# Top-k masks from one pass of signs: a change to the mask chain of a hybrid encoder kernel

## The chip, the cores and the metric

The kernel runs on one core of a Trainium2 chip. The metric is the device time of one execution in microseconds (us). TensorE is PE in the profile, its weight load PEld, VectorE is DVE, ScalarE is ACT, GpSimd is POOL, and SP issues the DMAs.

## The reference

The reference is an encoder trunk of two layers over 1024 tokens of width 1024, f32. Each layer has a token mixer (a gated convolution, six heads of sparse attention chosen by an indexer, six heads of chunked band attention), a cross-attention to 256 memory tokens, and a squared-ReLU MLP, each behind a layer norm. The change touches the choice of keys in the sparse attention:

```python
score = jnp.einsum('bqh,bqhs->bqs', iwb, jax.nn.relu(logits)).astype(jnp.float32)
admissible = key_chunk[None, :] <= q_chunk[:, None]
score = jnp.where(admissible[None], score, -jnp.inf)
_, idx = lax.top_k(score, topk)        # topk = 256 keys per query
...
s = jnp.einsum('bqhd,bqkd->bhqk', qb, k_sel).astype(jnp.float32) * scale
p = jax.nn.softmax(s, axis=-1)
```

Of equal scores, the top-k takes those with the lower index.

## The kernel before

Queries are worked in eight blocks of 128, one query per partition. Block b may see keys 0 to 128(b+1) - 1, so its scores have w = 128(b+1) columns. Blocks 0 and 1 see at most 256 keys and need no choice; blocks 2 to 7 (w = 384 to 1024) do.

The kernel keeps all keys and adds a mask before the softmax: 0 where a key is chosen, 2^100 (`BIG`) where not. `softmax` (L964) works on negated scores, takes the minimum of score plus mask along the way out of PSUM (L977), and applies Exp on ScalarE (L983).

`topk` (L761) makes the masks. It finds each query's threshold bit by bit, 32 rounds. Two groups of blocks are searched side by side: group 0 (blocks 7 and 6) counts on ScalarE, as the sum of Sign(threshold - score) (L789); group 1 (blocks 5 to 2) counts on VectorE (L793). Then the masks are made block by block, the narrowest first: 384, 512, 640, 768, 896 and 1024 columns. For the two blocks of group 0 some instructions ahead (L828 to L843) correct the threshold. Then, for every block:

- `eq` = BIG where the score equals the threshold (L845);
- the scores are overwritten by 1 where they are at or below the threshold, with their count (L848, whose accumulator is read by an instruction of its own);
- `need`, the number of equal scores still to be taken, times BIG (L853);
- `pre`, the running sum of `eq` (L856, a scan);
- `eq` is cleared where the running sum exceeds `need` (L857);
- the mask is written in bf16 over the scores' buffer (L860).

All are VectorE instructions. A block's mask is first read when sparse attention reaches that block, which is behind all 24 units of chunked attention.

Around it, `build` runs two streams side by side: the indexer followed by `topk`, and the projections, the convolution (L940, L943), and then the attention units. The instructions are put in order by the Tile framework's scheduler, by priorities: `topk` is emitted with a priority shifted by 3000 and the indexer by -2000. The order of each engine's queue is fixed when the kernel is compiled. `chunk_prepare` gets a head's queries and keys ready for chunked attention (ScalarE L1012 and L1021, VectorE L1013, GpSimd L1022, two DMAs L1017 and L1018 between halves of partitions, and the bias by a DMA, L1009, negated at L1026), its scores are made by L1054 and leave the two score banks through L977. Buffers in SBUF come from one arena of 52736 columns of 4 bytes, which gives out the place freed longest ago. Weights are loaded ahead by SP, cast on ScalarE (L285) and split on GpSimd (L286). L340 to L342 are the three matmuls of a product in split f32.

Of the kernel before, what the change touches and what calls it, by code (L numbers as in the profile page):

```python
# [15 lines left out]
BF16 = mybir.dt.bfloat16  # L16
I32 = mybir.dt.int32
AF = mybir.ActivationFunctionType
ALU = mybir.AluOpType
# [3 lines left out]
S = 1024  # L23
# [9 lines left out]
TOPK = 256  # L33
# [4 lines left out]
BIG = 2.0**100  # L38
# [272 lines left out]
class Kern:  # L311
# [449 lines left out]
    def topk(self, st):  # L761


        nc, sb = self.nc, self.sb


        groups = GROUPS
        junk, junk_a = sb.alloc(512), sb.alloc(512)
        tmp = [sb.alloc(S) for _ in range(2)]
        junkb = junk.ap.bitcast(BF16)  # L770
        junka = junk_a.ap.bitcast(BF16)
        col = sb.alloc(len(groups) * 32)
        state = []
        for g, blocks in enumerate(groups):

            state.append(
                [col.ap[:, g * 32 + 8 * i : g * 32 + 8 * i + len(blocks)] for i in range(3)]
            )
            nc.gpsimd.memset(state[g][0], 0.0)

        for bit in range(31, -1, -1):
            for g, blocks in enumerate(groups):
                cand, gone, cnt = state[g]
                ci, gi = cand.bitcast(I32), gone.bitcast(I32)
                for j, b in enumerate(blocks):
                    w = (b + 1) * P
                    x, c, n = st["score"][b].ap, cand[:, j : j + 1], cnt[:, j : j + 1]
                    if g == 0:
                        nc.scalar.activation(  # L789
                            junka[:, :w], x, AF.Sign, bias=c, scale=-1.0, accum_out=n  # L790
                        )
                    else:
                        nc.vector.tensor_scalar(  # L793
                            junkb[:, :w], x, c, None, op0=ALU.is_ge, op1=ALU.add, accum_out=n
                        )

                back = -1.0 if bit == 31 else float(1 << bit)
                if g == 0:
                    for j, b in enumerate(blocks):
                        nc.vector.tensor_scalar(  # L800
                            gi[:, j : j + 1], cnt[:, j : j + 1],
                            float((b + 1) * P - 2 * TOPK), back, op0=ALU.is_gt, op1=ALU.mult,
                        )
                else:
                    nc.vector.tensor_scalar(
                        gi, cnt, float(TOPK), back, op0=ALU.is_lt, op1=ALU.mult
                    )

                if bit == 31:
                    nc.vector.tensor_scalar(ci, gi, 1 << 30, None, op0=ALU.bitwise_xor)  # L810
                else:
                    nc.vector.scalar_tensor_tensor(  # L812
                        ci, gi, 1 << (bit - 1) if bit else 0, ci,
                        op0=ALU.bitwise_xor, op1=ALU.bitwise_xor,
                    )
                yield TP * len(blocks) / 4
        for g, blocks in list(enumerate(groups))[::-1]:
            fl, cnt = state[g][0], state[g][2]
            for j, b in list(enumerate(blocks))[::-1]:
                w = (b + 1) * P  # L820
                sc = st["score"][b]
                tcol = fl[:, j : j + 1]
                eq, pre = (x.ap[:, :w] for x in tmp)
                if g == 0:


                    above, more = self.small(1), self.small(1)
                    nc.vector.tensor_scalar(  # L828
                        eq, sc.ap, tcol, None, op0=ALU.is_gt, op1=ALU.add,
                        accum_out=cnt[:, j : j + 1],  # L830
                    )
                    nc.vector.tensor_scalar(
                        eq, eq, -HIGH, HIGH, op0=ALU.mult, op1=ALU.add
                    )
                    nc.vector.tensor_tensor_reduce(
                        pre, sc.ap, eq, 1.0, HIGH, op0=ALU.add, op1=ALU.min,
                        accum_out=above,
                    )
                    nc.vector.tensor_scalar(
                        more.bitcast(I32), cnt[:, j : j + 1], float(TOPK), None,  # L840
                        op0=ALU.is_ge,
                    )
                    nc.vector.copy_predicated(tcol, more.bitcast(I32), above)  # L843

                nc.vector.tensor_scalar(  # L845
                    eq, sc.ap, tcol, BIG, op0=ALU.is_equal, op1=ALU.mult
                )
                nc.vector.tensor_scalar(  # L848
                    sc.ap, sc.ap, tcol, None, op0=ALU.is_le, op1=ALU.add,
                    accum_out=cnt[:, j : j + 1],  # L850
                )
                need = self.small(1)
                nc.vector.tensor_scalar(  # L853
                    need, cnt[:, j : j + 1], float(TOPK - w), BIG, op0=ALU.add, op1=ALU.mult
                )
                nc.vector.tensor_tensor_scan(pre, eq, eq, 0.0, op0=ALU.add, op1=ALU.max)  # L856
                nc.vector.scalar_tensor_tensor(  # L857
                    eq, pre, need, eq, op0=ALU.is_le, op1=ALU.mult
                )
                nc.vector.scalar_tensor_tensor(  # L860
                    sc.mask, sc.ap, BIG, eq, op0=ALU.mult, op1=ALU.subtract
                )
                sb.free(sc.high, self.w.late)
                yield 4.0
        for x in [junk, junk_a, col] + tmp:
            sb.free(x, self.w.late)

    def dsa_proj(self, l, xt, st):
# [1230 lines left out]
```

## Time and profile before

| what | value |
|---|---|
| median of 3 runs | 3052.46 us (3051.95 to 3061.31) |
| the profiled execution | 3054.18 us |
| its span on the core | 3052.4 us |
| mean granted TensorE clock | 0.973 |
| PE busy | 2894.9 us, 95% |
| DVE busy | 2239.0 us, 73% |
| ACT busy | 1527.2 us, 50% |
| POOL busy | 1317.6 us, 43% |

The span is that of the profiled execution, from its first instruction to its last; its own time is 1.8 us longer. Busy shares are means over the whole span. The mask chains run from 267 to 331 us in the first layer and from 1788 to 1858 us in the second.

### The profile page before, as it was taken

What the parts mean: (1) busy time and instruction counts of PE and PEld (TensorE: products, weight loads), DVE (VectorE), ACT (ScalarE), POOL (GpSimd) and SP (SyncE); (2) the same over time, 40 slices, a digit from 0 to 9 for tenths busy, and PEclk for the clock granted to TensorE, in tenths of its full rate; (3) what the DMA queues carried; (4) which work ended last, traced back from release to release, by engine and by line L of the source; (5) the groups of instructions that cost most, each with busy time, mean ns of one, the idle gap of its engine ahead of it and who ended that gap; (6) DMA issues with size and microseconds to landing.
All of it is one profiled execution on the core that took longest, in us unless ns stands there. A gap on an engine that the chain in (4) does not pass through costs nothing. (4 is left out here: it accounts for less than half of the span.)

```text
span 3052.4 us, 43458 instructions
## 1 busy us (share of the span) xinstructions
PE 2894.9 (95%) x14440; PEld 2452.0 (80%) x14440; DVE 2239.0 (73%) x4423; ACT 1527.2 (50%) x3074; POOL 1317.6 (43%) x1260
## 2 busy tenths in 40 slices
PE   8998799999999999999998987999999999999998
PEld 7886688878877788888787866887888777888886
DVE  5899978672478776777858998785725877667787
ACT  5676766513324455544456757665232344554442
POOL 4615566522335553232455154665223355532223
PEclk9999899999999999999999998999999999999999
DMA  3212133331325446755322121323312354466553
GB/s 125 55 43 57 50 102 113 116 114 39 105 101 175 165 154 223 247 186 189 123 71 55 39 65 41 116 93 125 114 52 101 110 174 162 152 249 227 182 180 115
DMA packets 261890, 374.14 MB, mean 123 GB/s; under 512 B 22560, under 2 KB 141344, under 8 KB 261664
## 3 DMA queue, kind: packets, MB, share of 16 engines
q1 hardware_dynamic: 261664, 371.35, 37.0%
q8 instruction: 114, 1.87, 0.2%
q14 instruction: 112, 0.92, 0.1%
HBM read 269.56 MB, written 95.42 MB: 120 GB/s over the span
## 5 line engine op out<-in xcount | busy, mean ns | idle before, releaser
L340 PE MATMUL banks<-sb,sb 128*128 128x512 f32 (+3 forms) x3776 | 1427.2, 379 | 31.8 <-DVE sb L645 11.7
L341 PE MATMUL banks<-sb,sb 128*128 128x512 f32 (+3 forms) x3776 | 1421.4, 377 | 6.0 <-POOL sb L286 5.9
L342 PE MATMUL banks<-sb,sb 128*128 128x512 f32 (+3 forms) x3776 | 1419.5, 377 | 6.5 <-POOL sb L645 6.5
L645 POOL TENSOR_TENSOR sb<-sb,sb 128x512 fp32r<-128x512 f32 (+1 forms) x428 | 588.1, 1386 | 946.1 <-ACT sb L644 834.9
L340 PEld LDWEIGHTS banks<-sb,sb 128*128 128x128 f32 x3776 | 717.0, 190 | 164.0 <-DVE sb L645 14.9
L342 PEld LDWEIGHTS banks<-sb,sb 128*128 128x128 f32 x3776 | 717.1, 190 | 132.0 <-POOL sb L645 7.3
L341 PEld LDWEIGHTS banks<-sb,sb 128*128 128x128 f32 x3776 | 717.6, 190 | 128.7 <-POOL sb L286 7.5
L644 ACT CAST sb<-sb 128x512 fp32r<-128x512 f32 (+1 forms) x788 | 452.5, 605 | 580.1 <-PE banks L341 135.1
L286 POOL TENSOR_TENSOR sb<-sb,sb 128x512 fp32r<-128x512 f32 (+2 forms) x288 | 376.3, 1319 | 512.0 <-ACT sb L285 403.7
L645 DVE TENSOR_TENSOR sb<-sb,sb 128x512 fp32r<-128x512 f32 x360 | 285.8, 821 | 41.6 <-ACT sb L644 41.3
L645 DVE TENSOR_TENSOR sb<-banks,sb 128x384 fp32r<-128x384 f32 (+2 forms) x324 | 187.8, 595 | 80.8 <-ACT sb L644 76.1
L644 ACT CAST sb<-banks 128x384 fp32r<-128x384 f32 (+2 forms) x324 | 160.0, 516 | 172.1 <-PE banks L1521 75.2
L793 DVE TENSOR_SCALAR_CACHE_REDUCE sb<-sb,sb 128x768 bf16<-128x768 f32 (+3 forms) x256 | 207.5, 811 | 4.9 <-POOL sb L749 2.3
L1685 DVE TENSOR_TENSOR sb<-sb,sb 128x512 f32<-128x512 f32 x160 | 158.4, 1025 | 56.9 <-ACT sb L1665 53.9
L1727 DVE TENSOR_TENSOR sb<-banks,sb 128x512 f32<-128x512 f32 x224 | 149.8, 683 | 45.9 <-PE banks L342 40.4
L983 ACT ACTIVATE sb<-sb,sb 128x640 f32<-128x640 f32 (+7 forms) x192 | 141.7, 739 | 77.5 <-DVE sb L977 73.2
L285 ACT CAST sb<-sb 128x512 fp32r<-128x512 f32 (+2 forms) x192 | 112.0, 599 | 125.9 <-PE banks L341 29.2
L994 POOL TENSOR_SCALAR sb<-sb,sb 128x128 f32<-128x128 f32 (+7 forms) x192 | 144.9, 770 | 66.6 <-DVE sb L992 60.6
L789 ACT ACTIVATE sb<-sb,sb 128x1024 bf16<-128x1024 f32 (+1 forms) x128 | 140.3, 1096 | 51.6 <-DVE sb L812 46.8
L1790 DVE TENSOR_TENSOR sb<-sb,sb 128x512 f32<-128x512 f32 x128 | 97.9, 767 | 70.5 <-DMA sb<-w_ff_dram 69.8
L1664 ACT ACTIVATE sb<-sb 128x512 f32<-128x512 f32 x128 | 80.7, 631 | 123.7 <-DVE sb L1727 123.5
L1582 DVE TENSOR_TENSOR sb<-sb,sb 128x512 f32<-128x512 f32 x96 | 91.6, 954 | 50.7 <-DMA h<-sb 30.7
(173 smaller groups left out, 3128.1 us busy)
## 6 DMA issues: line engine op xcount, KB each, us to landing
sb<-h SPq DMA_DIRECT2D x236, 256.0 KB, 3.1
h<-sb SPq DMA_DIRECT2D x224, 256.0 KB, 2.1
sb<-w_ff_dram SPq DMA_DIRECT2D x216, 256.0 KB, 3.1
sb<-w_ff_dram SPq DMA_DIRECT2D x64, 512.0 KB, 4.4
sb<-w_in_dram SPq DMA_DIRECT2D x64, 256.0 KB, 2.8
sb<-w_mkv_dram SPq DMA_DIRECT2D x64, 256.0 KB, 2.7
xs<-sb SPq DMA_DIRECT2D x24, 512.0 KB, 2.6
sb<-xs SPq DMA_DIRECT2D x24, 512.0 KB, 3.8
```

The lines of the kernel that those rows point to most:

```text
L286: k.nc.gpsimd.tensor_tensor(lo, st, hi.bitcast(F32), op=ALU.subtract)
L340: mm(out, lh, rh, start=start, stop=False)
L341: mm(out, lh, rl, start=False, stop=False)
L342: mm(out, ll, rh, start=False, stop=stop)
L644: nc.scalar.copy(hi, src)
L645: eng.tensor_tensor(lo, src, hi.bitcast(F32), op=ALU.subtract)
L789: nc.scalar.activation(junka[:, :w], x, AF.Sign, bias=c, scale=-1.0, accum_out=n)
L793: nc.vector.tensor_scalar(junkb[:, :w], x, c, None, op0=ALU.is_ge, op1=ALU.add, accum_out=n)
L983: nc.scalar.activation(pt.ap, pt.ap, AF.Exp, bias=mn, scale=-1.0, accum_out=sm)
L994: nc.gpsimd.tensor_scalar(pt.ap, pt.ap, rc[:, i : i + 1], 0.0, op0=ALU.mult, op1=ALU.add)
L1685: nc.vector.tensor_tensor(z.ap, x, y, op=ALU.add if spec[1] == "+" else ALU.subtract)
L1727: nc.vector.tensor_tensor(r.ap, ps.ap, part[c, x].ap, op=ALU.add)
```

## The change

The chain from the corrected threshold on is replaced. One pass on ScalarE writes the signs of (threshold - score) in bf16, +1 below the threshold, 0 at it, -1 above, and their sum. VectorE then makes 1 where the sign is 0 (bf16), its running sum, and 4096 times the sign plus the running sum; one comparison of that with `need` writes the mask. `need`, now without BIG, is computed by two one-column instructions from the last running sum and the total of the signs. The scores are no longer overwritten before the mask is. Two buffers of 512 columns, for signs and equalities, are held for as long as `topk` runs, and serve all blocks in turn.

```diff
@@ topk
         tmp = [sb.alloc(S) for _ in range(2)]
+        half = [sb.alloc(512) for _ in range(2)]
...
+                side, same = (x.bitcast(BF16)[:, :w] for x in (half[0].ap, half[1].ap))
+                total, need = self.small(1), self.small(1)
+                nc.scalar.activation(
+                    side, sc.ap, AF.Sign, bias=tcol, scale=-1.0, accum_out=total
+                )
+                nc.vector.tensor_scalar(same, side, 0.0, None, op0=ALU.is_equal)
+                nc.vector.tensor_tensor_scan(pre, same, same, 0.0, op0=ALU.add, op1=ALU.max)
+
                 nc.vector.tensor_scalar(
-                    eq, sc.ap, tcol, BIG, op0=ALU.is_equal, op1=ALU.mult
+                    need, pre[:, w - 1 : w], total, 0.5, op0=ALU.add, op1=ALU.mult
+                )
+                nc.vector.tensor_scalar(need, need, float(TOPK - w // 2), None, op0=ALU.add)
+                nc.vector.scalar_tensor_tensor(
+                    pre, side, 4.0 * S, pre, op0=ALU.mult, op1=ALU.add
                 )
                 nc.vector.tensor_scalar(
-                    sc.ap, sc.ap, tcol, None, op0=ALU.is_le, op1=ALU.add,
-                    accum_out=cnt[:, j : j + 1],
-                )
-                need = self.small(1)
-                nc.vector.tensor_scalar(
-                    need, cnt[:, j : j + 1], float(TOPK - w), BIG, op0=ALU.add, op1=ALU.mult
-                )
-                nc.vector.tensor_tensor_scan(pre, eq, eq, 0.0, op0=ALU.add, op1=ALU.max)
-                nc.vector.scalar_tensor_tensor(
-                    eq, pre, need, eq, op0=ALU.is_le, op1=ALU.mult
-                )
-                nc.vector.scalar_tensor_tensor(
-                    sc.mask, sc.ap, BIG, eq, op0=ALU.mult, op1=ALU.subtract
+                    sc.mask, pre, need, BIG, op0=ALU.is_gt, op1=ALU.mult
                 )
...
-        for x in [junk, junk_a, col] + tmp:
+        for x in [junk, junk_a, col] + tmp + half:
             sb.free(x, self.w.late)
```

## Rows read from the trace of the kernel before

**Rows 1.** The page, busy time by engine: us, share of the span, instructions.
```profile
PE 2894.9 (95%) x14440; PEld 2452.0 (80%) x14440; DVE 2239.0 (73%) x4423; ACT 1527.2 (50%) x3074; POOL 1317.6 (43%) x1260
```
**Rows 2.** Windows: stretch, its length, busy us of each engine, clock, DMA share, GB/s.
```profile
core 0: us, PE busy (x) PEld busy (x) DVE busy (x) ACT busy (x) POOL busy (x), PEclk, DMA share, GB/s
...
267.00:285.00 18.00, 17.49 (x78) 14.14 (x76) 17.82 (x31) 10.52 (x21) 9.44 (x7) 1.00 0.15 44
...
285.00:331.00 46.00, 21.67 (x88) 16.36 (x88) 45.31 (x70) 19.52 (x38) 33.82 (x23) 0.69 0.24 59
1800.00:1859.00 59.00, 36.29 (x143) 28.53 (x142) 56.73 (x105) 27.97 (x58) 40.66 (x36) 0.71 0.21 53
...
285.00:314.00 29.00, 11.91 (x39) 8.81 (x39) 28.41 (x41) 13.75 (x26) 28.18 (x18) 0.68 0.35 86
...
330.00:400.00 70.00, 60.92 (x389) 52.84 (x389) 61.28 (x192) 60.11 (x145) 35.85 (x51) 0.90 0.23 62
```
**Rows 3.** TensorE in order of time, first layer: start, us, instruction, idle before it, releaser.
```profile
289.21 0.77 PE L1054 MATMUL banks<-sb,sb 128*128 128x128 f32 x2 [4.72 <-DVE sb L1013]
...
296.34 0.39 PE L1054 MATMUL banks<-sb,sb 128*128 128x128 f32 x2
304.80 3.72 PE L1054 MATMUL banks<-sb,sb 128*128 128x384 f32 x8 [8.07 <-DVE sb L977]
...
331.94 1.50 PE L1054 MATMUL banks<-sb,sb 128*128 128x320 f32 x4 [7.28 <-DVE sb L977]
```
**Rows 4.** VectorE in order of time, first layer.
```profile
267.31 0.42 DVE L845 TENSOR_SCALAR sb<-sb,sb 128x384 f32<-128x384 f32 x1
...
304.45 0.28 DVE L977 CUSTOM_DVE_ANT_0 sb<-banks,sb 128x128 f32<-128x128 f32 x1
...
330.13 1.22 DVE L860 SCALAR_TENSOR_TENSOR sb<-sb,sb 128x1024 bf16<-128x1024 f32 x1
```
**Rows 5.** VectorE's mask lines, all widths together: count, busy us, mean ns, idle before.
```profile
L856 DVE TENSOR_TENSOR_SCAN sb<-sb 128x384 f32<-128x384 f32 (+5 forms) x12 | 20.7, 1727 | 0.0
...
L860 DVE SCALAR_TENSOR_TENSOR sb<-sb,sb 128x384 bf16<-128x384 f32 (+5 forms) x12 | 15.5, 1289 | 0.1
L857 DVE SCALAR_TENSOR_TENSOR sb<-sb,sb,sb 128x384 f32<-128x384 f32 (+5 forms) x12 | 15.3, 1272 | 0.2
L848 DVE TENSOR_SCALAR_CACHE_REDUCE sb<-sb,sb 128x384 f32<-128x384 f32 (+5 forms) x12 | 11.3, 943 | 0.2
L845 DVE TENSOR_SCALAR sb<-sb,sb 128x384 f32<-128x384 f32 (+5 forms) x12 | 10.1, 845 | 0.2
...
L853 DVE TENSOR_SCALAR sb<-sb 128x1 f32<-128x1 f32 x12 | 1.7, 138 | 0.0
...
L848 DVE DVE_READ_ACCUMULATOR sb<-sb,sb 128x1 f32 x12 | 1.0, 82 | 0.0
```
**Rows 6.** The same engine's lines with widths kept apart.
```profile
L793 DVE TENSOR_SCALAR_CACHE_REDUCE sb<-sb,sb 128x768 bf16<-128x768 f32 x64 | 64.8, 1012 | 4.2 <-POOL sb L749 2.3
...
L845 DVE TENSOR_SCALAR sb<-sb,sb 128x768 f32<-128x768 f32 x2 | 3.1, 1526 | 0.1
...
L848 DVE TENSOR_SCALAR_CACHE_REDUCE sb<-sb,sb 128x768 f32<-128x768 f32 x2 | 2.0, 1012 | 0.0
...
L845 DVE TENSOR_SCALAR sb<-sb,sb 128x640 f32<-128x640 f32 x2 | 1.1, 554 | 0.0
...
L845 DVE TENSOR_SCALAR sb<-sb,sb 128x384 f32<-128x384 f32 x2 | 0.8, 421 | 0.1
```
**Rows 7.** ScalarE's lines with widths kept apart.
```profile
L789 ACT ACTIVATE sb<-sb,sb 128x1024 bf16<-128x1024 f32 x64 | 73.6, 1149 | 50.2 <-DVE sb L812 46.8 <-DVE sb L805 1.5 <-DVE sb L810 0.9
L789 ACT ACTIVATE sb<-sb,sb 128x896 bf16<-128x896 f32 x64 | 66.7, 1042 | 1.3
...
L983 ACT ACT_TABLE_LOAD x1 | 1.3, 1283 | 0.0
```
**Rows 8.** ScalarE in order of time, first layer.
```profile
279.62 0.62 ACT L285 CAST sb<-sb 128x512 fp32r<-128x512 f32 x1 [4.84 <-DVE sb L943]
...
300.09 0.74 ACT L1026 ACTIVATE sb<-sb 128x640 f32<-128x640 f32 x1 [5.65 <-DMA sb<-rel_ext_dram]
```

## The prediction

> **What bounds the kernel now.** I read the page first. TensorE is busy 95% of the span [rows 1], so a change on VectorE can pay only where TensorE stands idle. The windows by stage say where that is. Before the masks TensorE is full, and from 330 on nearly so; between, from 285 to 331 in the first layer it works 21.7 us of 46, and from 1800 to 1859 in the second 36.3 of 59 [rows 2]: 24.3 + 22.7 = 47 us without work. In both stages VectorE is full (45.3 of 46, 56.7 of 59) and ScalarE is not (19.5 and 28.0). The reader is to see that VectorE is the bound for a stage of some 50 us per layer, in a kernel that TensorE bounds elsewhere.
>
> The order of time shows that it is VectorE's queue that holds TensorE. TensorE waits 4.72 us for the low halves of a query (L1013), then 8.07 and 7.28 us for the maxima that clear a score bank (L977) [rows 3]. The bank of the first was written by the matmuls at 296.3, and its L977 ran at 304.45 behind mask work. VectorE runs from the first mask instruction at 267.3 to the last, which ends at 331.3, and TensorE moves again at 331.9 [rows 3, 4]. No mask is needed there, since the 24 units of chunked attention come first; the masks only stand ahead of them in the queue. So a microsecond taken out of this queue is one that TensorE can get back, until 47 are used up.
>
> **The change part by part.** Twelve mask chains run, six widths in each of two layers, 384 to 1024 columns. Removed, in the sums over all twelve: equality in f32 (L845) 10.1, the counting comparison (L848) 11.3 and its accumulator read 1.0, need (L853) 1.7, scan (L856) 20.7, comparison with need (L857) 15.3, the mask's combination (L860) 15.5 [rows 5]: 75.6 us.
>
> In their place, on VectorE:
> - Scan: same length, two operands that are the same tensor, now bf16. I leave it at 20.7.
> - Equality on bf16 signs, writing bf16. No row shows it. It can't cost less than the twelve one-column instructions of L853, 1.7, and hardly more than the f32 form, 10.1. The f32 form runs 421 ns at 384 columns and 554 at 640 where nothing disturbs it [rows 6], so 0.52 ns a column on a fixed 222 ns. Half the bytes per operand make me expect something nearer the middle: 5.0. By the Trainium skill (VectorE: DVE Perf Modes, the perf-mode tier table) a one-source operation on bf16 in SBUF takes half the cycles per element of f32; 12 fixed parts and half the slope over 8448 columns would then be about 4.9, an estimate, so no run of before shows it and the sum would stay.
> - Two one-column instructions for need instead of one: 24 x 0.138 = 3.3.
> - The sum of running count and 4096 signs: two tensors as in L857, 15.3.
> - The comparison that writes the mask: one tensor and a column, the kind of L845, 10.1; at worst it is like L860, 15.5; at best like the bf16 equality's floor, 1.7.
>
> That is 20.7 + 5.0 + 3.3 + 15.3 + 10.1 = 54.4, a saving of 21.2 us. With both unknowns at their dear end it is 75.6 - 64.9 = 10.7, with both at the cheap end 75.6 - 42.7 = 32.9.
>
> The new wait is on ScalarE. Signs of 1024 and 896 columns run 1149 and 1042 ns [rows 7]; at 107 ns per 128 columns the six widths sum to 5.3 us, 10.6 for both layers, and the accumulator read, which only need waits for, is hidden behind the scan. ScalarE is busy under half of the stage, so its own time costs nothing there; without that cover it would be the 10.6. But the equality waits for the signs, and there is one buffer of signs, so a block's pass can't begin before the sum of the block before it is done. During the pass VectorE has that block's last comparison (10.1/12 = 0.84 us) and whatever else stands in its queue; between zero and 10.6 is exposed. I take half, 5.3, since about half of VectorE's time in the stage is other work that can fill the gap. Behind the waiting equality stand the next L977 and L1013, and TensorE waits for those. The function tables cost nothing: the trace has one load for Exp in all, and the second layer's signs run after it with none of their own [rows 7].
>
> 21.2 - 5.3 = 15.9 us of queue. Not all comes through: the two narrow blocks of each layer run while TensorE is still full (17.5 of 18 from 267 to 285 [rows 2]), and their saving pays only as far as the queue hands it on. I count three quarters, 11.9; between 8 and all of it is open. The two sign buffers take 1024 of 52736 columns while the search runs; I give that nothing: one wait in this stage, of 4.84 us, looks like one for a buffer [rows 8], and one more or fewer lies inside the range.
>
> The profiled execution took 3054.2, so 3042.3; the median of the runs shown is 1.7 lower, which makes **3040.6 us**.
>
> **The rivals.**
> *The port shared with GpSimd keeps the time.* From 285 to 314 GpSimd is as full as VectorE, 28.2 of 29 us [rows 2]. The equality at 768 columns took 1526 ns against 554 at 640, while the counting comparison at 768 took 1012, just what the search's comparison of 768 columns (L793) takes over its 64 runs [rows 6]. So one kind waits for GpSimd there, and the pass that is removed outright is of the other kind. If both engines are bound by a common path, only the time of the waiting kind pays: equality 5.1 and the mask 5.4, less 5.3 for the signs, at three quarters 3.9: 3048.6, no measurable change. The Trainium skill (SBUF — State Buffer, two separate sides) has it that VectorE in a two-port mode, or with two SBUF inputs, and GpSimd exclude each other for whole instructions; the rows above agree in kind. Against this rival: from 314 on GpSimd is free, and in the second layer it is only 40.7 of 59 busy [rows 2].
>
> *The order of the queue.* VectorE's order is settled at compile time. If the first L977 stays behind as many microseconds of masks as now, with further blocks moved in front of it, the savings on the four narrow blocks don't shorten TensorE's first waits. The two wide blocks of each layer are 45% of the columns, so 0.45 x 15.9 = 7.2 us come through: 3045.3. For it speaks that this L977 was ready 8 us before it ran; against it that the queue has no gap up to 331.
>
> *The signs get stuck in ScalarE's queue (slower).* ScalarE too works in order, and in this stage it stands behind others: 4.84 us until L943 was done, 5.65 us for the transfer of the bias [rows 8]. A sign pass queued behind such a wait stops VectorE, which had no gap before. For the three wide blocks of each layer that is six places; at 5.2 us each 31 us against 21.2 saved, so 10 us slower: 3062. It decides from 21.2/6 = 3.5 us per place. Against it: the thresholds of the first four blocks are there early, and one of these two waits ends with VectorE's own progress, so VectorE can't be far ahead of it.
>
> **How the numbers follow.** Forecast 0.5 (its own range 3030 to 3045), port 0.2, order 0.12, signs stuck 0.18. A measurement here can tell about 0.3%, 9.2 us, from no change. Faster by more than that: nearly all of the forecast and a little of the port and order cases, 0.5. Within: most of the port and order cases and the rest of the forecast, 0.3. Slower: 0.2. The low end takes the forecast with all 21.2 us coming through (3031.3) and some of the cheap price: 3027. The high end takes the stuck signs: 3062. A sixth lies outside.
>
> TensorE's clock may add to a gain: it was granted 0.69 of full speed from 285 to 331 and 0.90 from 330 to 400, where TensorE had stood idle, against 1.00 before [rows 2], a mixture of 1.2 and 2.4 GHz. If it came back at once, up to 10% of 61 us per layer; I leave it out of the sum and in the low end.
>
> **What would show it.** VectorE's mask lines should sum to about 54 us, the equality near 0.4 us, the last comparison like L845. VectorE from the first mask instruction to the last should take some 56 us instead of 64 in layer one, and TensorE's idle time in the two stages about 35 us instead of 47. If the equality's idle time before it names the sign pass with more than 3.5 us a time, or L977 still makes TensorE wait 8 and 7 us, I am wrong. If GpSimd's instructions grow as VectorE's shrink, it is the port. If the gain in both stages is there and the end doesn't move, it was given back behind 400.

## The result and the profile after

The changed kernel takes 3028.5 us (median of 4 runs, 3024.13 to 3032.82) against 3053.51 (4 runs) for the kernel before: a ratio of 0.9913, 95% interval 0.9888 to 0.9938. That is 25 us less. The forecast was 3040.6, 11.9 us less than the median shown: the direction is right, the time lies in the range, but the gain is twice what was forecast and outside the forecast case's own range of 3030 to 3045. The profiled execution took 3024.74 us.

The page after, span and busy time by engine, which answers [rows 1]:

```profile
span 3022.8 us, 43484 instructions
...
PE 2887.8 (96%) x14440; PEld 2445.2 (81%) x14440; DVE 2215.3 (73%) x4411; ACT 1536.3 (51%) x3098; POOL 1325.8 (44%) x1260
```

VectorE is busy 23.7 us less over the span, of which not all need be the change's: two traces of the kernel before differ by 7.3 (2239.0 here, 2231.7 in e13 below). Line numbers after: sign pass L848, equality L851, scan L852, `need` L854 and L857, sum L858, last comparison L861; names further down stand one line later than before (L977 is L978).

VectorE's mask lines after, and ScalarE's sign pass, all widths together, against [rows 5]; columns as there:

```profile
L852 DVE TENSOR_TENSOR_SCAN sb<-sb 128x384 f32<-128x384 bf16 (+5 forms) x12 | 22.5, 1876 | 0.2
L858 DVE SCALAR_TENSOR_TENSOR sb<-sb,sb 128x384 f32<-128x384 bf16 (+5 forms) x12 | 15.6, 1300 | 0.0
L861 DVE TENSOR_SCALAR sb<-sb,sb 128x384 bf16<-128x384 f32 (+5 forms) x12 | 13.3, 1108 | 0.1
L851 DVE TENSOR_SCALAR sb<-sb 128x384 bf16<-128x384 bf16 (+5 forms) x12 | 7.7, 644 | 1.4 <-ACT sb L848 1.4
L854 DVE TENSOR_SCALAR sb<-sb,sb 128x1 f32<-128x1 f32 x12 | 2.5, 208 | 0.1
L857 DVE TENSOR_SCALAR sb<-sb 128x1 f32<-128x1 f32 x12 | 1.8, 148 | 0.1
...
L848 ACT ACTIVATE sb<-sb,sb 128x384 bf16<-128x384 f32 (+5 forms) x12 | 10.5, 876 | 3.7 <-DVE sb L858 2.4 <-DVE sb L844 1.3
```

They sum to 63.4 us against 75.6: a saving of 12.2, not 21.2. Every line but the sum is clearly dearer than forecast. The wait for the signs, forecast at 5.3, is 1.4 in all, in 4 of 12 places.

VectorE in order of time after, first layer, against [rows 4]:

```profile
267.25 0.26 DVE L851 TENSOR_SCALAR sb<-sb 128x384 bf16<-128x384 bf16 x1 [0.25 <-ACT sb L848]
...
303.93 0.28 DVE L978 CUSTOM_DVE_ANT_0 sb<-banks,sb 128x128 f32<-128x128 f32 x1
...
331.92 1.00 DVE L861 TENSOR_SCALAR sb<-sb,sb 128x1024 bf16<-128x1024 f32 x1
```

From the first mask instruction to the end of the last it is 65.7 us, where 56 was forecast and 64.0 was before. TensorE in order of time after, against [rows 3], shows what has moved into that stretch:

```profile
288.22 0.47 PE L1055 MATMUL banks<-sb,sb 128*128 128x128 f32 x2 [3.04 <-DVE sb L1014]
...
304.27 1.01 PE L1055 MATMUL banks<-sb,sb 128*128 128x384 f32 x2 [9.87 <-DVE sb L978]
305.94 1.75 PE L1055 MATMUL banks<-sb,sb 128*128 128x512 f32 x4 [0.66 <-DVE sb L978]
310.06 2.42 PE L1055 MATMUL banks<-sb,sb 128*128 128x320 f32 x6 [2.36 <-DVE sb L978]
...
323.59 1.04 PE L1055 MATMUL banks<-sb,sb 128*128 128x512 f32 x4 [0.83 <-DVE sb L978]
...
326.91 0.96 PE L1106 MATMUL banks<-sb,sb 128*128 128x128 f32 x6 [2.11 <-DVE sb L645]
```

The first long wait is still there, and longer (9.87 for 8.07), but the pause of 7.28 us at the end of the masks is gone: TensorE works through it in short waits. Windows after over the stretches of [rows 2], and one more:

```profile
core 0: us, PE busy (x) PEld busy (x) DVE busy (x) ACT busy (x) POOL busy (x), PEclk, DMA share, GB/s
...
285.00:331.00 46.00, 25.28 (x109) 20.71 (x108) 44.63 (x86) 27.57 (x56) 35.05 (x31) 0.71 0.25 63
1800.00:1859.00 59.00, 45.65 (x215) 36.54 (x213) 53.98 (x138) 38.04 (x84) 39.99 (x38) 0.75 0.20 53
...
330.00:400.00 70.00, 63.61 (x456) 56.18 (x456) 64.78 (x202) 60.78 (x147) 42.00 (x58) 0.99 0.26 73
```

By these windows TensorE is idle 20.7 + 13.4 = 34 us instead of 47, but the second is not like for like: after the change the second layer's masks end at 1843.55, so 15 us of the window lie behind them. In the stretch that corresponds to it, 1787.8 to 1844.3, TensorE works 37.28 of 56.50 us, which makes 20.7 + 19.2 = 40 us idle for 47. Behind the first layer's masks the granted clock is 0.99 from 330 to 400 where it was 0.90.

**Where the 25 us came from.** I cut each layer's stage at three points: the end of the search's last counting comparison on VectorE (L793, after L794), the end of the last mask comparison, and the last output copy of chunked attention on ScalarE (L1116, after L1117). The kernel before, both layers:

```profile
265.80:331.35 65.55, 40.36 (x171) 31.51 (x169) 64.65 (x104) 31.09 (x59) 44.30 (x29) 0.78 0.21 54
331.35:440.20 108.85, 100.18 (x702) 90.78 (x703) 88.49 (x279) 85.58 (x215) 64.42 (x86) 0.95 0.28 83
1787.40:1858.20 70.80, 48.62 (x197) 38.72 (x195) 68.03 (x131) 35.54 (x72) 42.92 (x36) 0.76 0.21 51
1858.20:1968.40 110.20, 98.54 (x676) 88.86 (x677) 87.04 (x260) 79.63 (x202) 68.00 (x87) 0.92 0.30 90
```

The kernel after:

```profile
265.10:332.92 67.82, 46.33 (x203) 37.91 (x201) 64.62 (x124) 45.22 (x92) 49.03 (x40) 0.80 0.22 56
332.92:428.90 95.98, 89.67 (x662) 80.86 (x663) 83.20 (x263) 79.63 (x201) 61.23 (x81) 1.00 0.34 99
1775.20:1843.55 68.35, 49.13 (x194) 38.19 (x193) 64.51 (x136) 45.02 (x96) 55.94 (x42) 0.75 0.23 60
1843.55:1939.40 95.85, 88.07 (x634) 79.81 (x633) 81.10 (x239) 73.07 (x181) 58.43 (x76) 0.97 0.35 101
```

The mask stretches take the same time, 136.4 and 136.2 us. The stretches behind them take 191.8 instead of 219.1: the whole gain stands there. The work taken off VectorE was not handed back as an earlier end of the masks; its place was filled with chunked attention's own instructions (45 score evictions, the runs of L977, between the search and the last mask instead of 30, counted in the two traces), so less was left behind. And what was left ran at a granted clock of 1.00 and 0.97 instead of 0.95 and 0.92.

### The profile page after: what moved, and what is told of

Same layout as the page of the kernel before. It is cut to its first block, busy times and chain, and to the rows that moved or that the text cites. A ratio compares the mean times of both kernels' runs of the same rounds, so it can differ in the third digit from the quotient of the medians.

```text
span 3022.8 us, 43484 instructions
## 1 busy us (share of the span) xinstructions
PE 2887.8 (96%) x14440; PEld 2445.2 (81%) x14440; DVE 2215.3 (73%) x4411; ACT 1536.3 (51%) x3098; POOL 1325.8 (44%) x1260
## 4 chain that ended last, share of the span: by engine, by line
PE 52%; DVE 8%; DMA 3%; issue 2%; POOL 2%; ACT 1%; DVEq 0%; POOLq 0%; ACTq 0%; SPq 0%
PE banks L340 16%; PE banks L342 16%; PE banks L341 16%; DVE sb L645 2%; DMA sb<-w_ff_dram 2%; PE banks L1214 1%; PE banks L1185 1%; POOL sb L645 1%; PE banks L1205 0%; PE banks L1106 0%; PE banks L628 0%; DVE sb L978 0%; DVE sb L617 0%; DVE sb L794 0%; PE banks L1092 0%
## 5 line engine op out<-in xcount | busy, mean ns | idle before, releaser
L645 POOL TENSOR_TENSOR sb<-sb,sb 128x512 fp32r<-128x512 f32 (+1 forms) x428 | 594.5, 1400 | 943.4 <-ACT sb L644 770.4
L794 DVE TENSOR_SCALAR_CACHE_REDUCE sb<-sb,sb 128x768 bf16<-128x768 f32 (+3 forms) x256 | 207.5, 810 | 4.4 <-POOL sb L749 1.6
L995 POOL TENSOR_SCALAR sb<-sb,sb 128x128 f32<-128x128 f32 (+7 forms) x192 | 143.1, 761 | 74.4 <-DVE sb L993 73.8
L790 ACT ACTIVATE sb<-sb,sb 128x1024 bf16<-128x1024 f32 (+1 forms) x128 | 140.3, 1096 | 41.5 <-DVE sb L813 37.1
```

Of the source, the lines that this page charges most:

```text
L645: eng.tensor_tensor(lo, src, hi.bitcast(F32), op=ALU.subtract)
L790: nc.scalar.activation(junka[:, :w], x, AF.Sign, bias=c, scale=-1.0, accum_out=n)
L794: nc.vector.tensor_scalar(junkb[:, :w], x, c, None, op0=ALU.is_ge, op1=ALU.add, accum_out=n)
L995: nc.gpsimd.tensor_scalar(pt.ap, pt.ap, rc[:, i : i + 1], 0.0, op0=ALU.mult, op1=ALU.add)
```

## The experiments

Below, T is the length of the whole stage (start of the search's last counting comparison to the last output copy, some half a microsecond longer than the cuts above), both layers summed, and "outside" is the span less T. VectorE's busy and idle time are those inside T, from windows like the two above. "Rows" are its mask lines. The ratio is to the kernel before on the same chip. Chips differed (3053 on one, 3059 to 3060 on the others for the kernel before), so medians are not compared across them.

| run | ratio [95%] | rows | T | VectorE busy | idle | outside |
|---|---|---|---|---|---|---|
| before | 1 | 75.6 | 356.5 | 309.3 | 47.2 | 2695.9 |
| after | 0.9913 [0.9888, 0.9938] | 63.4 | 329.0 | 294.4 | 34.6 | 2693.8 |
| e1_buffers | 0.9987 [0.9977, 0.9996] | 77.8 | 353.1 | 314.4 | 38.7 | 2703.9 |
| e2_detour | 1.0006 [0.9996, 1.0015] | 84.2 | 359.3 | 314.8 | 44.5 | 2699.8 |
| e3_no_count | 0.9970 [0.9959, 0.9982] | 69.9 | 343.2 | 305.1 | 38.1 | 2699.9 |
| e4_equal_scores | 0.9927 [0.9912, 0.9942] | 66.7 | 340.2 | 300.1 | 40.1 | 2698.8 |
| e5_after_plus | 0.9936 [0.9921, 0.9950] | 74.0 | 338.3 | 303.2 | 35.1 | 2699.0 |
| e6_before_plus | 1.0035 [1.0021, 1.0049] | 94.4 | 363.6 | 322.3 | 41.3 | 2715.2 |
| e7_minus_two | 0.9902 [0.9885, 0.9918] | 54.7 | 325.8 | 289.3 | 36.5 | 2693.9 |
| e8_after_again | 0.9906 [0.9890, 0.9921] | 63.2 | 329.7 | 295.6 | 34.1 | 2696.0 |
| e9_places | 0.9943 [0.9928, 0.9957] | 65.7 | 328.8 | 294.5 | 34.3 | 2708.8 |
| e10_lower | 0.9913 [0.9897, 0.9930] | 63.2 | 330.6 | 296.2 | 34.4 | 2701.7 |
| e11_square | 0.9929 [0.9909, 0.9948] | 51.2 | 339.5 | 288.3 | 51.2 | 2696.5 |
| e12_before_places | 1.0006 [0.9996, 1.0016] | 80.0 | 349.8 | 312.7 | 37.1 | 2706.4 |
| e13_before_again | one run | 75.6 | 356.8 | 307.4 | 49.4 | 2703.2 |

The same program repeats T within 0.7 us on two chips (before and e13, after and e8), while its time outside the stage differs by 2 to 7. So T reads small effects, and the ratio says whether they reach the end. For e6 the profiled execution was the slowest of ten, 11.6 us above their median.

**The buffers alone, and the head of the chain.** e1 is the kernel before with the change's two buffers, unused:

```diff
         tmp = [sb.alloc(S) for _ in range(2)]
+        half = [sb.alloc(512) for _ in range(2)]
```

> The kernel before with the two buffers of 512 columns held through the search and not used; the mask chain is that of before. If the gain of 25 us is one of places in the arena, most of it is here: about 3030. If it comes from VectorE's work or from the order of its queue, the time stays at 3053, give or take 5.

e2 adds to that a sign pass ahead of the five old passes, whose equality now waits for it through one column:

```diff
+                total, held = self.small(1), self.small(1)
+                nc.scalar.activation(
+                    pre, sc.ap, AF.Sign, bias=tcol, scale=-1.0, accum_out=total
+                )
+                nc.vector.scalar_tensor_tensor(
+                    held, total, 0.0, tcol, op0=ALU.mult, op1=ALU.add
+                )
                 nc.vector.tensor_scalar(
-                    eq, sc.ap, tcol, BIG, op0=ALU.is_equal, op1=ALU.mult
+                    eq, sc.ap, held, BIG, op0=ALU.is_equal, op1=ALU.mult
```

> The chain of before, all five passes on VectorE, but held at its head by a pass of signs on ScalarE into the buffer of the running sum (so each block's pass waits for the block before it, as in the changed kernel) and a one-column instruction that hands the threshold on; the two idle buffers stay. VectorE's work is that of before and 12 one-column instructions (2 us), ScalarE's that of the changed kernel. If the gain is work taken from VectorE's full queue, this is no faster than before: 3053 to 3063. If it is the order of the queue (the wait for ScalarE lets the score evictions in between the pieces of a chain), most of the gain is here: 3030 to 3040.

The buffers alone give 0.13%, 4 us, a small part of 0.87. In e1 VectorE's order already changes (42 evictions ahead of the last mask, counted as above, instead of 30), and T falls by only 3.4; e2 has 46 and e6 (below) 45, and neither is faster than before. So more evictions ahead of the last mask do not make the gain by themselves. Against e1 the changed kernel's mask stretches are 6.9 us shorter and what lies behind them 17.2. With the sign pass ahead and nothing taken off VectorE, the gain is nil: the holding instruction itself took 6.0 us over twelve, and T rose by 6.2 against e1. The wait for ScalarE at the head is not what makes the kernel faster.

**One pass fewer, two fewer, one more.** e3 is e1 without the counting pass, e7 without the comparison with `need` as well, e6 is e1 with a second, unused count, and e5 is the changed kernel with an unused count. In the diff the first and third edits are those of e3, all but the last are those of e7, and the last is that of e5 and e6.

```diff
-                nc.vector.tensor_scalar(
-                    sc.ap, sc.ap, tcol, None, op0=ALU.is_le, op1=ALU.add,
-                    accum_out=cnt[:, j : j + 1],
-                )
...
-                nc.vector.scalar_tensor_tensor(
-                    eq, pre, need, eq, op0=ALU.is_le, op1=ALU.mult
-                )
...
-                    sc.mask, sc.ap, BIG, eq, op0=ALU.mult, op1=ALU.subtract
+                    sc.mask, sc.ap, 0.0, eq, op0=ALU.mult, op1=ALU.subtract
...
+                nc.vector.tensor_scalar(
+                    junkb[:, :w], sc.ap, tcol, None, op0=ALU.is_le, op1=ALU.add,
+                    accum_out=cnt[:, j : j + 1],
+                )
```

> The chain of before without the counting pass (12.3 us less on VectorE, accumulator reads included; need is computed from an old count and the mask from zero times the score, so the masks are not the reference's), with no wait for ScalarE; the two idle buffers stay. The time removed is what the changed kernel's rows removed, 12.2 us. If work is the cause: 3025 to 3040, as the changed kernel. If order is the cause: 3044 to 3053.

> The changed kernel with the counting pass of before put back as a pass that nothing uses (12.3 us more on VectorE, reads included, on top of its 63.4). If the end moves with VectorE's mask time, about 1.2 to 1.7 us for each, as the first four runs hint: 15 to 20 us slower than the changed kernel, 0.996 to 0.998 of before. If the gain hangs on the form of the new chain and the order that it gets, little is lost: 0.990 to 0.993 of before.

> The kernel before (with the two idle buffers) with one more counting pass that nothing uses, 12.3 us more on VectorE. If the end moves with VectorE's mask time: 15 to 20 us slower than before, 1.005 to 1.007. If the queue is not what counts: within 0.2% of before.

> The kernel before (with the two idle buffers) without the counting pass and without the comparison with need (28 us less on VectorE by the rows of before; the masks are not the reference's). If the end moves with VectorE's mask time at 1.2 to 1.7: 33 to 47 us faster, 0.985 to 0.989. If the order of the new chain is what counts: not better than without the counting pass alone, 0.997.

In order of dose, rows, T and time (the ratios' difference times 3060) against the kernel that each was made from: e7 -23.1, -27.3, -26; e3 -7.9, -9.9, -5; e5 against e8 +10.8, +8.6, +9; e6 +16.6, +10.5, +15. Summed without signs that is 58.4 us of mask rows and 55 us of time, 0.94 for one; from the intervals in the table each time is uncertain by 5 to 6 us and the 0.94 by about 0.18. Both ways, a microsecond more or less in the same chain is worth about one at the end, and there is no sign yet of a floor at 23 us saved. None of the four fell into the range that its expectation gave for VectorE's mask time as the cause: that took 1.2 to 1.7 for one, and the single doses gave 0.66 to 1.13. e5 (0.9936) came closest to the other range, that for the form of the new chain (0.990 to 0.993).

The rows are not the whole of it. e5 has 74.0 us of mask rows, 1.6 less than the kernel before and 3.8 less than e1, and is still 16 us faster than e1 (0.9936 for 0.9987). e8 is 25 us faster than e1 for 14.6 us of rows. So with the new chain, or with the order of the queues that comes with it, there are some 11 us that its rows do not account for. They are not TensorE working faster. From the pages of e1, e5 and e8, in this order:

```profile
PE 2897.1 (95%) x14440; PEld 2450.0 (80%) x14440; DVE 2236.7 (73%) x4423; ACT 1529.8 (50%) x3074; POOL 1324.1 (43%) x1260
...
PE 2895.8 (95%) x14440; PEld 2451.7 (81%) x14440; DVE 2221.7 (73%) x4435; ACT 1541.0 (51%) x3098; POOL 1327.3 (44%) x1260
...
PE 2889.8 (96%) x14440; PEld 2444.9 (81%) x14440; DVE 2217.4 (73%) x4411; ACT 1537.7 (51%) x3098; POOL 1322.1 (44%) x1260
```

e5's span is 19.7 us shorter than e1's, and TensorE, with the same 14440 matmuls, is busy only 1.3 us less: the rest is idle time of TensorE that is gone.

**Equality from the scores.** e4 is the changed kernel, but the equality reads the f32 scores and so doesn't wait for the signs:

```diff
-                nc.vector.tensor_scalar(same, side, 0.0, None, op0=ALU.is_equal)
+                nc.vector.tensor_scalar(same, sc.ap, tcol, None, op0=ALU.is_equal)
```

> The changed kernel with the equality taken from the scores instead of the signs, so that the head of the chain doesn't wait for ScalarE; only need and the sum with 4096 signs do. The equality reads f32: some 2 to 3 us more on VectorE over twelve blocks. If work is the cause: 3028 to 3034. If the wait at the head makes the order: a good part of the gain is lost, 3038 to 3053.

The equality costs 12.5 us, 4.8 more than from bf16 signs; rows rise by 3.5 against e8, T by 10.5, time by 0.21% (6 us); its 3037.5 us lie between the two ranges of its expectation. Most of the gain is there without the wait at the head. That T rises by three times the rows is not explained by the rows; more than half of it is idle time of VectorE (34.1 to 40.1), whose cause was not traced.

**The same again, other places, a lower priority.** e8 is the changed kernel once more. e9 allocates `half` ahead of `junk`, which moves later buffers, and e12 does the same to e1; e10 gives the mask chains a priority lower by another 6000, from the start of a chain to its end (the last two lines of the diff); e13 is the kernel before, run once: 3061.79 us, where the kernel before had a median of 3058.86 on that chip.

```diff
+        half = [sb.alloc(512) for _ in range(2)]
         junk, junk_a = sb.alloc(512), sb.alloc(512)
...
-        half = [sb.alloc(512) for _ in range(2)]
...
+                self.tc.cur_priority += 6000
...
+                self.tc.cur_priority -= 6000
```

> The changed kernel itself once more, beside the others on one chip: 0.991 of before, give or take 0.002.

> The changed kernel with its two buffers taken before the other two of the search, so that much of what is allocated later lies in other places. If the gain is VectorE's time in the stage: within 4 us of the changed kernel, 0.990 to 0.992 of before. If a good part of it is luck with the places: anything between 0.991 and 0.999.

> The changed kernel with its mask chains emitted at a priority lower by a further 6000, so that the scheduler lets the attention's instructions go first wherever both are ready. If TensorE's waits come from masks that stand ahead of evictions, it is faster than the changed kernel by some of the 40 us that TensorE still idles in the stages: 0.983 to 0.990. If VectorE's total time bounds the whole stage up to the last unit of chunked attention, whichever of its instructions goes first, it gains little: 0.989 to 0.992.

> The chain of before with two idle buffers taken ahead of the other two of the search, so in the places of the run that moved the buffers of the changed kernel: the two are a pair, as the run with idle buffers and the changed kernel are. If the chain itself gives a fixed gain in the stage from the end of the search to the last unit of chunked attention, the stage takes some 350 to 356 us here against 328.8 with the new chain, and what lies outside differs from that run by under 6 us; the whole then stands at 1.002 to 1.006 of before. If places make the gain, the stage is near 335 here too and the whole near 0.997.

> The kernel before itself, for a second trace on the chip of the other runs: the stage from the end of the search to the last unit of chunked attention 352 to 358 us, VectorE busy in it 309 to 315, outside it 2694 to 2704.

The gain repeats (e8). In e9 T is the same to a microsecond, but the kernel is 0.37% slower than e8, outside the range that its expectation gave for VectorE's time alone, and 12.8 us of its span have appeared outside the stage, in work that the change does not touch. e12's stage came out close to what was expected (349.8), its ratio a little below (1.0006 for 1.002 or more); e13's T repeats, with VectorE busy 307.4 where 309 or more was expected. At like places the change is worth 0.9906/0.9987, 25 us of 3060, or 0.9943/1.0006, 19 us. So where the buffers lie moves the end by 6 us (e12 against e1) to 11 us (e9 against e8). The order of VectorE's, ScalarE's and GpSimd's instructions differs between e9 and e8 as well, so it need not be the places themselves; which transfer or wait does it was not traced. e10 leaves T and time where they were, and shows nothing about priorities: in its trace the instructions of TensorE, VectorE, ScalarE and GpSimd come in the same order as in e8, all of them. It is the changed kernel a third time. Whether the gain would grow if evictions went ahead of masks stays untested.

**Equality on ScalarE.** e11 takes the equality off VectorE too: ScalarE squares the signs, and the scan adds ones and subtracts the squares.

```diff
+        one = sb.alloc(512)
+        nc.gpsimd.memset(one.ap.bitcast(BF16), 1.0)
...
-                nc.vector.tensor_scalar(same, side, 0.0, None, op0=ALU.is_equal)
-                nc.vector.tensor_tensor_scan(pre, same, same, 0.0, op0=ALU.add, op1=ALU.max)
+                nc.scalar.activation(same, side, AF.Square)
+                nc.vector.tensor_tensor_scan(
+                    pre, one.ap.bitcast(BF16)[:, :w], same, 0.0, op0=ALU.add, op1=ALU.subtract
+                )
```

> The changed kernel with one pass less on VectorE: ScalarE squares the signs, and the scan adds ones and takes the squares away, which gives the same running count. VectorE loses the equality, 7.7 us by its row, ScalarE gains twelve passes of some 0.8 us, and the chain waits for two passes instead of one. If the end moves with VectorE's time one for one: 7 to 9 us faster than the changed kernel, 0.988. If the wait for ScalarE begins to tell: 0.990 or slower.

VectorE's rows fall by 12 us and its busy time by 7.3 against e8, yet T is 9.8 longer and the ratio no better: idle time rises from 34.1 to 51.2. Its waits on VectorE in the second layer's stage (total us, times, longest) say whom it waits for:

```profile
engine line waited for: us in total, times, longest us
DVE sb L1018 <- ACT sb L1017: 5.1, 1, 5.1
DVE sb L285 <- DMA sb<-w_mo_dram: 5.0, 2, 2.5
...
DVE sb L803 <- ACT sb L792: 2.1, 2, 1.1
```

L1017 is ScalarE's copy of a query, L792 the search's sign pass. In the first layer the same two waits are 2.9 and 4.1. Together 14.2 us against 3.2 in the kernel after (1.0 + 0.3 + 1.6 + 0.3), so 11 of the 16.6 us that its idle time is above that kernel's. ScalarE in order of time ahead of the longest of them:

```profile
1794.96 1.13 ACT L1026 CAST sb<-sb 64x512 fp32r<-64x512 f32 x2
1795.99 0.72 ACT L850 ACTIVATE sb<-sb,sb 128x512 bf16<-128x512 f32 x1
...
1796.82 1.13 ACT L1026 CAST sb<-sb 64x512 fp32r<-64x512 f32 x2
1797.98 0.59 ACT L962 COPY sb<-banks 128x512 f32<-128x512 f32 x1
1798.59 0.62 ACT L285 CAST sb<-sb 128x512 fp32r<-128x512 f32 x1
1799.24 1.06 ACT L1017 ACTIVATE sb<-sb 64x1024 fp32r<-64x1024 f32 x1
```

The queue ahead of the query's copy has no gap, and a sign pass with its accumulator's read (L850) makes 0.9 us of it. This is akin to the slower rival: ScalarE's queue does hold VectorE, but what is late is not the sign but other work on ScalarE. How much of the 14.2 us the twelve squares cause, and how much the other order, was not separated. No version that does the whole work was faster than the changed kernel.

## Why the prediction was right in kind and wrong in size

**The bound was right.** VectorE holds a stage in each layer while TensorE has room, and a microsecond in or out of its queue is about one at the end (e3, e5, e6, e7 together). TensorE's idle time in the two stages fell less than forecast, to 40 us and not 35. That the time lies inside the stated range is in part luck: its low end stood on 21.2 us saved in the rows and all of it coming through, and 12.2 were saved.

**The step that failed** is the last one of the sum: three quarters of the rows saved, less the new wait, were taken for the whole gain, the two buffers were given nothing, and no term stood for what the new chain does beyond its own rows. The rows measured 12.2 saved and 1.4 of new wait, so 10.8; three quarters of that is 8.1, where 25 were measured. In its place the runs showed:

- A share of about 0.94, give or take 0.18, so that 0.75 lies at its edge. With it the 10.8 make 10 us; the rows saved against e1, which holds the same buffers, are 14.6 and make 14. The reason given for the discount, that the narrow blocks run while TensorE is full, is not borne out: the time came back behind the last mask. There VectorE still works 88.5 us of 108.9 and 87.0 of 110.2, beside a TensorE that works 100.2 and 98.5, and evictions that move up among the masks are gone from there.
- The buffers, given nothing: 4 us (e1), in places where they helped; in other places nothing (e12).
- A rest of 11 us (e8 against e1) or 6 (e9 against e12), and 12 in e5. Its cause stays open. The table splits T: from e1 to e8 it falls by 23.4, of which the mask rows are 14.6, VectorE's other instructions 4.2 and its idle time 4.6; from e12 to e9 by 21.0, of which 14.3, 3.9 and 2.8. The wait at the head is not the cause: e2 has it and gains nothing, and e4, without it, keeps a rest of 8 (18 us against e1 for 11.1 us of rows). The order of the queues, which is another one in each of these programs, may be: no run held it fixed, and e9 and e8, with the same work, differ by 11 us.
- The clock, named by the prediction and kept for its low end, is a small part. Over the span TensorE is busy 7.1 us less after the change (2887.8 for 2894.9), with the same 14440 matmuls, while the span is 29.6 us shorter; from e1 to e8 it is 7.3 of 31.3, from e1 to e5 1.3 of 19.7. What a higher clock gave back would show in that busy time, and it is no addition to the 0.94, in which each run's clock is already contained. Behind the masks e12 was granted 0.98 and 0.96, and it is no faster than before. No run changed the clock alone.

**The terms inside the sum** were off as well, and in opposite directions: saving 12.2 for 21.2, exposed signs 1.4 for 5.3. They net to 10.8 against 15.9, so the sum was too high where the path's share was too low. Of the saving's 9.0 us, the last comparison is 3.2, the equality 2.7, the scan 1.8, `need` 1.0, the sum 0.3. Two equalities, from VectorE's order of time after, and the instructions of GpSimd beside them show what makes the equality dear:

```profile
272.23 1.39 DVE L851 TENSOR_SCALAR sb<-sb 128x512 bf16<-128x512 bf16 x1
...
280.75 0.33 DVE L851 TENSOR_SCALAR sb<-sb 128x640 bf16<-128x640 bf16 x1 [0.16 <-ACT sb L848]
```

GpSimd in order of time after:

```profile
271.89 1.57 POOL L286 TENSOR_TENSOR sb<-sb,sb 128x512 fp32r<-128x512 f32 x1 [0.73 <-ACT sb L285]
...
278.84 1.41 POOL L286 TENSOR_TENSOR sb<-sb,sb 128x512 fp32r<-128x512 f32 x1 [1.81 <-ACT sb L285]
281.37 4.14 POOL L1023 TENSOR_TENSOR sb<-sb,sb 64x512 fp32r<-64x512 f32 x2 [1.13 <-ACT sb L1022]
```

The narrower equality, issued inside an instruction of GpSimd, took 1.39 us and ended 0.16 us behind it; the wider one, in GpSimd's gap from 280.25 to 281.37, took 0.33. Seven of the twelve took 0.24 to 0.43 and sum to 2.3, the other five, all beside instructions of GpSimd, sum to 5.4. Taking each width at its undisturbed time, twelve would be about 4.1, an estimate (768 columns put between its neighbours), so the wait beside GpSimd added some 3.6 us. With the Trainium skill (VectorE: DVE Perf Modes, the perf-mode tier table), whose bf16 `tensor_scalar` runs at twice the rate of f32, the prediction estimated 4.9 for all twelve; the undisturbed ones come out a little under it, and the measured sum of 7.7 is above it by the waits. The last comparison does the same: 1.34 and 1.45 us at 384 columns beside GpSimd, 0.54 at 640 columns in a gap.

**The rivals.** The port: contention is real, as these rows show, and took much of the saving in the rows, but it did not hold the gain at 3.9 us. The removed count, which was not of the waiting kind, is 12.3 us by its rows; taken out in e3 it gave 5 us at the end, put in it cost 9 in e5 and 15 in e6, each give or take 5 to 6. In e3 the scan and the comparison with `need` took 6.0 us longer than in e1 (25.0 and 18.8 for 21.8 and 16.0), half of what was taken out. The order of the queue: the first L978 is indeed as late as before (303.93 for 304.45), but the gain was not held to the two wide blocks' 7.2 us. Stuck signs: 1.4 us for a price of 31; other work stuck on ScalarE shows only in e11.

**What was expected in the profile.** "Some 56 us from first to last mask" was wrong (65.7): evictions filled the time; "L977 still makes TensorE wait 8 us" did happen once (9.87) and was no sign of failure. Moving the buffers, given nothing, is worth up to 0.37% (e9 against e8), 11 us, as much as the whole gain that was forecast.

## What to carry to other kernels

When an engine's queue bounds a stage, find the stage's end by where that engine's work for it ends, not by where the edited instructions end: time saved in the middle is refilled and shows up behind. Price a VectorE instruction twice, free and beside GpSimd, and sum by what GpSimd does at that time. Before crediting a change of a fraction of a per cent, run the kernel before with the same buffers allocated and unused, and put the work that was removed back into the new form: what then is left of the gain is not that work's. After a change of priority, compare the order of the instructions before reading its time.

## What the runs showed of the hardware

- A bf16 equality of 384 to 1024 columns took 0.24 to 0.43 us in seven places out of twelve, and 0.53 to 1.39 in five, all beside an instruction of GpSimd. The Trainium skill (SBUF — State Buffer, two separate sides) describes such an exclusion of VectorE and GpSimd for whole instructions; the pair of rows above agrees with it. Not every instruction of GpSimd did this: the equality at 1820.05 us ran in 0.38 with L995 recorded on GpSimd from 1819.96 to 1821.69.
- The scan did not gain from bf16 operands: 22.5 us for twelve, where f32 operands gave 20.7 (before) to 25.0 (e3). In the first layer it took 0.96 us at 384 columns and 2.28 at 1024, the f32 form 0.95 and 2.29.
- A one-column instruction with another column as operand (L854) took 208 ns, one with constants alone (L857) 148.
